# A hybrid decoder layer on one core: the up-projection by Strassen's seven products of quarters

## The chip, the core and the metric

The kernel runs on one core of a Trainium2 chip. A core has TensorE (PE: matmuls; PEld are its weight loads, which overlap them), VectorE (DVE), ScalarE (ACT), GpSimd (POOL) and SyncE (SP), which here issues nearly all DMAs. Each engine works through its own instructions in the order of the program and waits for others by semaphores. The metric is the device time of one execution in microseconds (us); lower is better.

## The reference, cut to what matters

One decoder layer is applied to a prompt of 2048 positions and a sample group of 8 x 4 positions, with shared weights. Everything is fp32. The change concerns the first matmul of the channel mixer:

```python
def conv_glu_ffn(x, conv_state, w_up, conv_w, conv_b, w_down):
    L = x.shape[1]
    a, g = jnp.split(x @ w_up, 2, axis=-1)        # w_up: 1024 x 5632
    ext = jnp.concatenate([conv_state.astype(a.dtype), a], axis=1)
    conv = conv_b
    for j in range(CONV_W):                        # CONV_W = 3
        conv = conv + ext[:, j:j + L] * conv_w[j]
    h = jax.nn.gelu(conv) * g
    return h @ w_down, ext[:, -(CONV_W - 1):]      # w_down: 2816 x 1024
```

Before it come a projection, a state-space scan, windowed attention, gates and a first layer norm; after it a second layer norm.

## The kernel before, in words

**Blocks.** The prompt is worked on in four blocks of 512 positions (`body`); block 1 also carries the 32 sample positions and has 544 columns. In each block the activations lie transposed (channels on partitions, positions along the row), so a weight tile of 128 x 128 is the stationary operand and 512 positions are the moving one.

**fp32 by three passes.** Every operand of a large matmul is split into a high part and the remainder, and a product is hi x hi + hi x lo + lo x hi. For weights, `Weights` does this: a *weight unit* is a tile of 128 x 1024 fp32 (512 KB); SP loads it into `wr` (3 buffers, line 192), ScalarE copies it to `wh`, and VectorE, or GpSimd for every third unit (line 202), subtracts to get `wl` (4 buffers each). `W.get` and `W.ahead` issue loads up to four units and splits up to three units ahead of the unit in use. `ws_unit` (line 226) issues a unit's matmuls (line 235).

**The channel mixer.** The 2816 channels are 22 *units* f of 128. Per f one weight unit makes the a half (`ua`) and one the g half (`ug`), 24 matmuls each (8 slices of the contraction x 3 passes). `ffn_tail` does the convolution (ScalarE's first tap and two VectorE operations) and gelu (square, a VectorE operation, tanh, a VectorE operation); between the two it calls `meanwhile`, which splits a weight unit. `ffn_gate` multiplies by g, splits a weight unit, and then splits the result into `hh` (ScalarE) and `hl` (VectorE). The f go in two groups, (0, 12) and (12, 22); after each the down-projection (`dn`, lines 239 to 241) takes the h of two f per weight unit and adds into z, once for each half of the 1024 output columns. `first_units` runs f = 0 and 1 in halves of 256 columns, because the positions of the second half are normalised later; `x1_evict` makes x1h and x1l, the parts of the normalised x1, by way of `x1f`.

**What sets the order.** The program's order is each engine's order. `Background` holds small steps with due times in *ticks*; `bg.tick()` is called after each weight unit or so and emits what is due: attention, the scan, tables, the rewriting of the residual rows by gain and bias (`x1_rows`, four GpSimd operations a row tile), the next block's input. In block 0 GpSimd also makes the scan's tables.

**Buffers.** All activations share one pool of 61 slots in SBUF; PSUM has 8 banks.

Of the kernel before, what the change touches and what calls it, by code (L numbers as in the profile page):

```python
# [8 lines left out]
F32 = mybir.dt.float32  # L9
# [15 lines left out]
SLOTS = 61  # L25
FU = 2
GROUPS = ((0, 12), (12, 22))
# [20 lines left out]
class Background:  # L48


    def __init__(self):
        self.now = 0
        self.todo = []
        self.n = 0
# [12 lines left out]
    def tick(self):  # L67
        due = sorted((x for x in self.todo if x[0] <= self.now), key=lambda x: (x[3], x[0], x[1], x[2]))
        self.todo = [x for x in self.todo if x[0] > self.now]
        self.now += 1  # L70
        for x in due:
            x[4]()

    def drain(self):
        while self.todo:
            self.tick()
# [3 lines left out]
def tile_hybrid_layer(ctx: ExitStack, tc: tile.TileContext,  # L80
# [4 lines left out]
    nc = tc.nc  # L85
# [47 lines left out]

    def unit_src(key):
# [27 lines left out]
        if k == "ug":  # L162
            return u_cols(w_up, 0, 8, DFF + key[1] * 128, 128)
        if k == "dn":
            return u_cols(w_down, (GROUPS[key[1]][0] + 2 * key[3]) * 128, 2, key[2] * 512, 512)
# [3 lines left out]
    for b in range(NBLK):  # L169
# [8 lines left out]
        for g, (f0, f1) in enumerate(GROUPS):  # L178
            for f in range(f0, f1):
                order += [("ua", f), ("ug", f)]  # L180
            order += [("dn", g, h, i) for h in range(2) for i in range((f1 - f0) // 2)]
# [1031 lines left out]
    def body(B, nxt):  # L1213
# [238 lines left out]
        x1l = {k: S("x1l", 544, F32R) for k in range(8)}  # L1452
        tps = {}
# [34 lines left out]
        def x1_evict(half):  # L1488
# [7 lines left out]
            f = [S("x1f") for _ in range(4)]  # L1496
            fk = lambda k: f[k // 2][:, (k % 2) * 256:(k % 2) * 256 + c]
# [40 lines left out]
        acc3 = wo_second(3)  # L1538
        upper, whole, lower = x1_evict(0)
# [22 lines left out]
        for i in range(B.nt):  # L1562
            bg.add(6 + 3 * i, lambda i=i: x1_rows(i))
        fst = Blk()

        def ffn_tail(f, pa, meanwhile):
# [3 lines left out]
            for i, c0, c in segs:  # L1570
                act(ae[:, 2 + c0:2 + c0 + c], pa[i][:, 0:c])
            G.tensor_copy(cc[:, :, f], ae[:, 512:514])  # L1572
# [5 lines left out]
            if B.sp:  # L1578
# [3 lines left out]
                act(ex[:, 16:48], pa[1][:, 256:288])  # L1582
# [5 lines left out]
            meanwhile()  # L1588
# [5 lines left out]
            fst.c = c_  # L1594
# [10 lines left out]
        def first_units():  # L1605
# [48 lines left out]
        for g, (f0, f1) in enumerate(GROUPS):  # L1654
# [8 lines left out]
            for f in range(f0 or 2, f1):  # L1663
                wa = [w.rearrange("p (k m) -> p k m", k=8) for w in W.get(("ua", f))]
                pa = ws_unit(*wa, 8, x1h, x1l, cols)
                ffn_tail(f, pa, W.ahead)
                bg.tick()
                wg = [w.rearrange("p (k m) -> p k m", k=8) for w in W.get(("ug", f))]
                pg = ws_unit(*wg, 8, x1h, x1l, cols)
                hh[f], hl[f] = ffn_gate(f, pg, W.ahead)  # L1670
                bg.tick()
            if g == 1:
                x1h.clear()
                x1l.clear()
                if nxt is not None:
# [9 lines left out]
                bg.add(3, lds)  # L1685
            for h in range(2):
# [14 lines left out]
                def dn_evict(t):  # L1701
# [7 lines left out]
                    if g == 1:  # L1709
# [4 lines left out]
                outer = 4 if B.last and g == 1 and h == 1 else 0  # L1714
                for i in range(nu - outer):
                    w = get(i)
                    for t in range(B.nt):
                        dn_mm(t, i, w)
                        if i == nu - 1:
                            dn_evict(t)  # L1720
                    bg.tick()
                if outer:
                    four = [get(nu - 4 + i, i) for i in range(4)]
                    for t in range(B.nt):
                        for i in range(4):
                            dn_mm(t, nu - 4 + i, four[i])
# [38 lines left out]

    B = new_block(0)
# [69 lines left out]
```

## Time and profile before

| | us |
|---|---|
| median of 3 runs | 2919.1 (2919.03 to 2923.91) |
| the profiled execution's own time | 2920.97 |
| its span, from the first to the last instruction | 2919.2 |

| engine | busy us | share |
|---|---|---|
| TensorE's weight loads | 2420.9 | 83% |
| VectorE | 1697.6 | 58% |
| ScalarE | 1142.5 | 39% |
| GpSimd | 1049.9 | 36% |

How to read it: busy time is the union of an engine's instructions over the span. Matmuls are pipelined, so the duration of one is longer than the distance to the next; the pace is read from starts or from counts in a stretch. PEclk is the granted share of TensorE's full clock. In a timeline, what stands in brackets behind a row is how long the engine was idle before it and what ended that.

### The profile page before, as it was taken

How to read it: one execution, taken by the hardware profiler on the slowest of the kernel's cores; microseconds unless marked ns; L12 is line 12 of the kernel's file. 1: busy time of each engine (PE TensorE's matmuls, PEld its weight loads, DVE VectorE, ACT ScalarE, POOL GpSimd, SP SyncE). 2: the span in 40 equal slices, each digit the busy share in tenths (PEclk: the TensorE clock that was granted, in tenths of full speed). 3: DMA queues.
4: the chain of work that ended last, by engine and by line, in shares of the span. 5: the costliest groups of instructions: out<-in, count | busy, mean ns of one | idle time of the engine just before them, and what ended most of it. 6: DMA issues, size and time to landing. Idle time of an engine off the chain costs nothing.

```text
span 2919.2 us, 39248 instructions
## 1 busy us (share of the span) xinstructions
PE 2843.7 (97%) x15168; PEld 2420.9 (83%) x15168; DVE 1697.6 (58%) x2678; ACT 1142.5 (39%) x1991; POOL 1049.9 (36%) x1098
## 2 busy tenths in 40 slices
PE   9899999999989999999999999999999999999998
PEld 8777888888888989989977778888888787888887
DVE  6975676254685447734646754673545853575365
ACT  3335344243326325423524442442433263344241
POOL 1955144111454313522217641351124651253122
PEclk9989999999999999999999999999999999999999
DMA  4422323234622242222325224233245423323232
GB/s 138 148 62 73 123 88 107 91 94 139 186 68 87 68 132 73 88 94 75 121 89 187 80 73 145 73 101 101 87 137 154 124 71 116 101 87 108 87 94 97
DMA packets 415118, 304.31 MB, mean 104 GB/s; under 512 B 52283, under 2 KB 351122, under 8 KB 414914
## 3 DMA queue, kind: packets, MB, share of 16 engines
q1 hardware_dynamic: 412114, 293.84, 33.0%
q0 software_dynamic: 2816, 7.96, 0.7%
q8 instruction: 119, 1.95, 0.3%
q14 instruction: 69, 0.57, 0.1%
HBM read 285.30 MB, written 17.39 MB: 104 GB/s over the span
## 4 chain that ended last, share of the span: by engine, by line
PE 82%; POOL 7%; DVE 6%; issue 2%; ACT 2%; DMA 0%; SPq 0%; POOLq 0%; DVEq 0%; ACTq 0%
PE ps L235 52%; PE ps L239 8%; PE ps L241 8%; PE ps L240 8%; PE ps L286 2%; POOL m L121 2%; POOL w L121 1%; PE ps L932 1%; POOL ht L121 1%; DVE m L121 1%; DVE m L776 1%; DVE wl L121 1%; POOL wl L121 1%; PE ps L247 1%; DVE x1l L121 0%
## 5 line engine op out<-in xcount | busy, mean ns | idle before, releaser
L121 POOL TENSOR_TENSOR wl<-wr,wh 128x1024 fp32r<-128x1024 f32 x144 | 358.5, 2490 | 991.1 <-ACT wh L113 957.9
L113 ACT ACTIVATE wh<-wr 128x1024 fp32r<-128x1024 f32 x448 | 470.4, 1052 | 292.3 <-PE ps L241 195.4
L235 PE MATMUL ps<-x1l,wh 128*128 128x512 f32 (+2 forms) x1856 | 569.4, 342 | 2.0 <-DVE x1l L121 2.0
L235 PE MATMUL ps<-x1h,wh 128*128 128x512 f32 (+2 forms) x1856 | 568.9, 342 | 0.0
L235 PE MATMUL ps<-x1h,wl 128*128 128x512 f32 (+2 forms) x1856 | 568.1, 341 | 0.0
L121 DVE TENSOR_TENSOR wl<-wr,wh 128x1024 fp32r<-128x1024 f32 x304 | 395.2, 1302 | 234.4 <-ACT wh L113 233.5
L235 PEld LDWEIGHTS ps<-x1l,wh 128*128 128x128 f32 x1856 | 326.4, 188 | 44.9 <-DVE x1l L121 3.0
L235 PEld LDWEIGHTS ps<-x1h,wl 128*128 128x128 f32 x1856 | 325.7, 188 | 41.8
L235 PEld LDWEIGHTS ps<-x1h,wh 128*128 128x128 f32 x1856 | 326.0, 188 | 41.3
L235 PE MATMUL ps<-xh,wh 128*128 128x512 f32 (+1 forms) x880 | 287.5, 358 | 11.7 <-DVE q L121 5.5
L235 PE MATMUL ps<-xh,wl 128*128 128x512 f32 (+1 forms) x880 | 281.6, 353 | 1.5 <-DVE wl L121 1.5
L235 PE MATMUL ps<-xl,wh 128*128 128x512 f32 (+1 forms) x880 | 281.8, 353 | 0.0
L239 PE MATMUL ps<-wh,hh 128*128 128x512 f32 x704 | 279.3, 397 | 0.0
L241 PE MATMUL ps<-wh,hl 128*128 128x512 f32 x704 | 277.9, 395 | 0.0
L240 PE MATMUL ps<-wl,hh 128*128 128x512 f32 x704 | 277.2, 394 | 0.0
L118 DVE SCALAR_TENSOR_TENSOR cv<-ae,pc,cv 128x512 f32<-128x512 f32 x176 | 145.7, 828 | 223.3 <-ACT cv L115 220.2
L235 PEld LDWEIGHTS ps<-xh,wh 128*128 128x128 f32 x880 | 157.7, 190 | 36.8 <-issue 5.9
L1572 POOL COPY cc<-ae 128x2 f32<-128x2 f32 x88 | 19.7, 224 | 468.1 <-ACT ae L113 467.3
L235 PEld LDWEIGHTS ps<-xh,wl 128*128 128x128 f32 x880 | 156.9, 190 | 25.4 <-DVE wl L121 2.5
L235 PEld LDWEIGHTS ps<-xl,wh 128*128 128x128 f32 x880 | 157.9, 190 | 20.9
L125 POOL TENSOR_SCALAR pp<-pp,su 128x256 f32<-128x256 f32 x128 | 143.6, 1139 | 84.0 <-DVE su L904 48.5
L239 PEld LDWEIGHTS ps<-wh,hh 128*128 128x128 f32 x704 | 132.7, 188 | 31.0
(363 smaller groups left out, 4966.4 us busy)
## 6 DMA issues: line engine op xcount, KB each, us to landing
wr<-in_w_up SPq DMA_DIRECT2D x176, 512.0 KB
wr<-in_w_in SPq DMA_DIRECT2D x88, 512.0 KB
wr<-in_w_down SPq DMA_DIRECT2D x88, 512.0 KB
wr<-in_w_glu SPq DMA_DIRECT2D x64, 256.0 KB
wr<-in_w_o SPq DMA_DIRECT2D x32, 512.0 KB
xin<-in_x_prompt SPq DMA_DIRECT2D x32, 256.0 KB
wr<-in_w_in SPq DMA_DIRECT2D x32, 256.0 KB
wr<-in_w_attn_br SPq DMA_DIRECT2D x32, 256.0 KB
```

The costliest lines, as they stand in the source:

```text
L113: A.activation(out, in_, AF.Copy, scale=scale, **kw)
L118: eng.scalar_tensor_tensor(out, a, s, b, op0=op0, op1=op1, **kw)
L121: eng.tensor_tensor(out, a, b, op=op)
L125: eng.tensor_scalar(out, a, s1, None, op0=op0)
L235: T.matmul(ps[:, :n], w[:, k, :], x[k][:, c0:c0 + n], start=(i == 0), stop=(i == len(ops) - 1))
L239: T.matmul(ps[:m], ah, wh, start=first, stop=False)
L240: T.matmul(ps[:m], ah, wl, start=False, stop=False)
L241: T.matmul(ps[:m], al, wh, start=False, stop=last)
L247: T.matmul(ps[:64], a, wh, start=first, stop=last)
L286: T.transpose(out, in_, ident[:k, :k])
L776: V.tensor_tensor_scan(v2[:, a, r, :], r4[:, gp:gp + 1].to_broadcast([128, 128]), v1[:, a, r, :], hc[:, r, gp:gp + 1], OP.mult, OP.add)
L932: T.matmul(B.ops[qb][r, :], vt[:, qb + kt, r], pt[kt], start=(kt == 0), stop=(kt == 1))
```

## The change

For 20 of the 22 units (f = 2 to 21) the up-projection of two neighbouring units becomes one *pair*. Its weights, 1024 x 256 for a and for g, are cut into quarters (halves of the contraction by the two units), the positions into two halves of 256 (272 in block 1); of the eight products of quarters Strassen's algorithm (the Winograd form) makes seven, three of plain quarters and four with sums of weights and of activations. A product takes one weight unit (its a and g parts, 4 slices each) and gives two PSUM banks of 256 columns; VectorE adds the products up. The sums of weights are made once, in the first ticks of the program, and kept in DRAM; the sums of x1 are made in each block by GpSimd and split like other operands. The activation tails of a pair are cut into six steps, which are emitted one per product of the next pair, or in the down-projection. There are four groups in place of two, and 65 slots.

```diff
-SLOTS = 61
+SLOTS = 65
-GROUPS = ((0, 12), (12, 22))
+GROUPS = ((0, 6), (6, 12), (12, 16), (16, 22))
+LG = len(GROUPS) - 1
+PRODUCTS = ("11", "21", "t4", "t1", "t2", "t3", "22")
...
+    def tick(self, draining=False):
...
+        if not draining:
+            next(self.steps, None)
...
+    def up_part(f, what, h):
+        r0, c0 = 512 * (what[0] == "2"), h * DFF + (f + (what[1] == "2")) * 128
+        return w_up[r0:r0 + 512, c0:c0 + 128].rearrange("(k p) m -> p k m", p=128)
+
+    def weight_sums():
+        for f in range(2, NF, 2):
+            for h in range(2):
+                v = {}
+                for what in ("11", "12", "21", "22"):
+                    v[what] = S("ws")
+                    SP.dma_start(v[what].rearrange("p (k m) -> p k m", k=4), up_part(f, what, h))
+                yield
+                tt(v["11"], v["12"], v["11"], OP.subtract, G)
+                tt(v["12"], v["22"], v["12"], OP.subtract, G)
+                tt(v["22"], v["22"], v["11"], OP.subtract, G)
+                tt(v["21"], v["21"], v["22"], OP.subtract, G)
+                yield
+                yield
+                for what, src in (("t1", "11"), ("t3", "12"), ("t2", "22"), ("t4", "21")):
+                    SP.dma_start(sums[f, what][:, h * 512:(h + 1) * 512], v[src])
+                del v
+                yield
...
-            bg.add(6 + 3 * i, lambda i=i: x1_rows(i))
+            bg.add(3 + 3 * i, lambda i=i: x1_rows(i))
...
+        def x1_sums():
+            for k in range(4):
+                s12, s34 = S("s12", 544), S("s34", 544)
+                lo_, hi_ = slice(0, hn), slice(hn, n)
+                tt(s12[:, lo_], x1f[k][:, hi_], x1f[k + 4][:, hi_], OP.add, G)
+                tt(s12[:, hi_], s12[:, lo_], x1f[k][:, lo_], OP.subtract, G)
+                tt(s34[:, lo_], x1f[k][:, lo_], x1f[k][:, hi_], OP.subtract, G)
+                tt(s34[:, hi_], x1f[k + 4][:, lo_], s12[:, hi_], OP.subtract, G)
+                for j, t in enumerate((s12, s34)):
+                    sh[j, k], sl_[j, k] = split(B, t, None, "s")
...
+        def tail():
+            if tails:
+                tails.pop(0)()
+
+        def pair(f):
...
+            for i in range(7):
+                hi, lo = (w.rearrange("p (h k m) -> p h k m", h=2, k=4) for w in W.get(("up", f, i)))
+                xh_, xl_ = operand(i)
+                ps[i] = [P()[:, 0:hn] for _ in range(2)]
+                for h in range(2):
+                    ws_unit(hi[:, h], lo[:, h], 4, xh_, xl_, [(0, hn)], ps[i][h:h + 1])
+                for h in range(2):
+                    c11, c12, c21, c22 = out(h, 0, 0), out(h, 1, 0), out(h, 0, hn), out(h, 1, hn)
+                    u = u2[:, h * hn:(h + 1) * hn]
+                    p_ = ps[i][h]
+                    if i == 0:
+                        act(u, p_)
+                    elif i == 1:
+                        tt(c11, u, p_, OP.add)
+                    elif i == 4:
+                        tt(u, u, p_, OP.add)
+                        tt(c12, u, ps[3][h], OP.add)
+                        tt(c21, u, ps[2][h], OP.add)
+                    elif i == 5:
+                        tt(c22, c12, p_, OP.add)
+                        tt(c21, c21, p_, OP.add)
+                    elif i == 6:
+                        tt(c12, c12, p_, OP.add)
...
+                W.ahead()
+                tail()
+                bg.tick()
...
+            for i in range(2):
+                tails.extend((lambda i=i: convolved(i), activated, lambda i=i: gated(i)))
...
                     for fn in x1_evict(1):
                         fn()
+                    x1_sums()
                 half0(i)
...
-            for f in range(f0 or 2, f1):
...
+            for f in range(f0 or 2, f1, 2):
+                pair(f)
...
-                        bg.add(2 + k, lambda k=k: x_split(nxt, k))
+                        bg.add(2 + k // 2, lambda k=k: x_split(nxt, k))
-                bg.add(3, lds)
+                bg.add(1, lds)
...
                         if i == nu - 1:
                             dn_evict(t)
+                    for _ in range(-(-6 // (nu - 1))):
+                        tail()
                     bg.tick()
...
+    bg.steps = weight_sums()
```

`convolved` is the convolution of `ffn_tail`, `activated` its gelu, and `gated` the multiplication by g and the split of `ffn_gate`; the weight splits that lay inside these functions are now in `W.ahead`, once per product. `x1f` is kept for whole rows until the sums are made. In the last block all steps of the last half down-projection, not four of five, are held and run position tile by position tile. The scratch space for DMA descriptors is set to 4096, which makes room for the slots.

## Rows read from the trace of the kernel before

**Rows 1.** The page's first part: busy us (share of the span) xinstructions, by engine.

```profile
PE 2843.7 (97%) x15168; PEld 2420.9 (83%) x15168; DVE 1697.6 (58%) x2678; ACT 1142.5 (39%) x1991; POOL 1049.9 (36%) x1098
```

**Rows 2.** Table of stretches: us, busy us and instructions by engine, PEclk, DMA share, GB/s.

```profile
2060.00:2160.00 100.00, 100.00 (x436) 81.35 (x435) 59.13 (x67) 47.39 (x64) 21.15 (x23) 1.00 0.34 105
2590.00:2670.00 80.00, 80.00 (x349) 65.03 (x348) 59.19 (x56) 38.26 (x52) 39.28 (x32) 1.00 0.34 104
2690.00:2742.00 52.00, 52.00 (x225) 42.06 (x224) 10.52 (x12) 9.54 (x9) 7.34 (x4) 1.00 0.29 91
...
1370.00:1450.00 80.00, 80.00 (x643) 80.00 (x642) 49.94 (x79) 39.00 (x72) 17.57 (x28) 1.00 0.29 89
```

**Rows 3.** Timeline of PE in the first units: start us, us, instruction.

```profile
2548.51 0.28 PE L235 MATMUL ps<-x1h,wh 128*128 128x256 f32 x1
...
2549.22 0.28 PE L235 MATMUL ps<-x1h,wh 128*128 128x256 f32 x1
```

**Rows 4.** The page's groups, weight loads: xcount, busy us, mean ns, idle before.

```profile
L235 PEld LDWEIGHTS ps<-x1l,wh 128*128 128x128 f32 x1856 | 326.4, 188 | 44.9 <-DVE x1l L121 3.0
```

**Rows 5.** Timeline of VectorE, additions of 256 columns from PSUM.

```profile
810.54 0.42 DVE L121 TENSOR_TENSOR m<-ps,tber 128x256 f32<-128x256 f32 x1
810.88 0.41 DVE L121 TENSOR_TENSOR m<-ps,tbei 128x256 f32<-128x256 f32 x1
```

**Rows 6.** Timelines of ScalarE and VectorE over one unit's tail, block 3.

```profile
2574.71 0.82 ACT L115 ACTIVATE cv<-ae,pc 128x512 f32<-128x512 f32 x1 [1.40 <-POOL ae L1569]
2577.13 0.63 ACT L115 ACTIVATE cq<-cv 128x512 f32<-128x512 f32 x1 [1.61 <-DVE cv L118]
2578.52 0.63 ACT L115 ACTIVATE cq<-cq 128x512 f32<-128x512 f32 x1 [0.76 <-DVE cq L118]
2579.06 1.04 ACT L113 ACTIVATE wh<-wr 128x1024 fp32r<-128x1024 f32 x1
2580.71 0.63 ACT L113 ACTIVATE hh<-cv 128x512 fp32r<-128x512 f32 x1 [0.60 <-DVE cv L118]
...
2575.56 1.54 DVE L118 SCALAR_TENSOR_TENSOR cv<-ae,pc,cv 128x512 f32<-128x512 f32 x2 [0.93 <-ACT cv L115]
2577.80 0.69 DVE L118 SCALAR_TENSOR_TENSOR cq<-cq,cv 128x512 f32<-128x512 f32 x1 [0.70 <-ACT cq L115]
2579.19 0.69 DVE L118 SCALAR_TENSOR_TENSOR cv<-cq,cv 128x512 f32<-128x512 f32 x1 [0.70 <-ACT cq L115]
2579.99 0.69 DVE L118 SCALAR_TENSOR_TENSOR cv<-cv,ps 128x512 f32<-128x512 f32 x1
2580.59 1.22 DVE L121 TENSOR_TENSOR wl<-wr,wh 128x1024 fp32r<-128x1024 f32 x1
2581.73 0.69 DVE L121 TENSOR_TENSOR hl<-cv,hh 128x512 fp32r<-128x512 f32 x1
```

**Rows 7.** Timelines of GpSimd and VectorE, block 2.

```profile
2085.08 2.40 POOL L121 TENSOR_TENSOR wl<-wr,wh 128x1024 fp32r<-128x1024 f32 x1 [5.60 <-ACT wh L113]
...
2086.26 1.76 DVE L121 TENSOR_TENSOR hl<-cv,hh 128x512 fp32r<-128x512 f32 x1 [0.70 <-ACT hh L113]
```

**Rows 8.** Groups by form, GpSimd, whole span.

```profile
L121 POOL TENSOR_TENSOR x1l<-x1f,x1h 128x256 fp32r<-128x256 f32 x16 | 14.2, 919 | 0.0
```

**Rows 9.** Table of stretches, mixer of block 0.

```profile
66.00:141.00 75.00, 71.02 (x423) 61.58 (x422) 69.68 (x104) 25.07 (x45) 70.24 (x110) 1.00 0.48 144
141.00:200.00 59.00, 48.18 (x236) 41.86 (x235) 53.39 (x78) 14.79 (x21) 39.23 (x49) 0.83 0.27 86
```

**Rows 10.** The page's third part: DMA queue, kind: packets, MB, share of 16 engines.

```profile
q1 hardware_dynamic: 412114, 293.84, 33.0%
```

**Rows 11.** Timeline of PE around a wait in block 2, and the table of stretches there.

```profile
1542.71 0.40 PE L239 MATMUL ps<-wh,xh 128*128 128x512 f32 x1
1548.50 0.81 PE L240 MATMUL ps<-wl,xh 128*128 128x512 f32 x1 [5.39 <-POOL wl L121]
...
1545.00:1552.00 7.00, 3.50 (x9) 2.88 (x10) 0.16 (x1) 0.00 (x0) 6.74 (x8) 0.51 0.33 92
```

More of the change, by code (lines that the diff above doesn't have):

```diff
@@ L51, in __init__ @@
     def __init__(self):
+        self.steps = iter(())
         self.now = 0
@@ L132, in u_cols @@
                            w[r0:r0 + 128 * kk, c0:c0 + m].rearrange("(k p) m -> p k m", p=128))]
+    sums = {}
+    for f in range(2, NF, 2):
+        for what in ("t1", "t2", "t3", "t4"):
+            sums[f, what] = dram.tile([128, 1024], F32, name=f"sum_{f}_{what}")
+    def up_part(f, what, h):
+        r0, c0 = 512 * (what[0] == "2"), h * DFF + (f + (what[1] == "2")) * 128
+        return w_up[r0:r0 + 512, c0:c0 + 128].rearrange("(k p) m -> p k m", p=128)
+    def weight_sums():
+        for f in range(2, NF, 2):
+            for h in range(2):
[14 more added lines that the diff above has]
+                yield
     def unit_src(key):
@@ L163, in unit_src @@
             return u_cols(w_up, 0, 8, DFF + key[1] * 128, 128)
+        if k == "up":
+            f, what = key[1], PRODUCTS[key[2]]
+            if what[0] == "t":
+                return lambda t: [(t, sums[f, what])]
+            return lambda t: [(t.rearrange("p (h k m) -> p h k m", h=2, k=4)[:, h], up_part(f, what, h))
+                              for h in range(2)]
         if k == "dn":
@@ L178, in tile_hybrid_layer @@
         for g, (f0, f1) in enumerate(GROUPS):
-            for f in range(f0, f1):
-                order += [("ua", f), ("ug", f)]
+            if g == 0:
+                order += [(n_, f) for f in range(2) for n_ in ("ua", "ug")]
+            for f in range(f0 or 2, f1, 2):
+                order += [("up", f, i) for i in range(7)]
             order += [("dn", g, h, i) for h in range(2) for i in range((f1 - f0) // 2)]
@@ L1495, in x1_evict @@
             sl = slice(c0, c0 + c)
-            f = [S("x1f") for _ in range(4)]
-            fk = lambda k: f[k // 2][:, (k % 2) * 256:(k % 2) * 256 + c]
+            fk = lambda k: x1f[k][:, sl]
             def affine(out, k):
@@ L1538, in body @@
         acc3 = wo_second(3)
+        x1f.update({k: S("x1f", 544) for k in range(8)})
         upper, whole, lower = x1_evict(0)
@@ L1571, in ffn_tail, with conv @@
                 act(ae[:, 2 + c0:2 + c0 + c], pa[i][:, 0:c])
+            conv(f, ae, pa[1][:, 256:288] if B.sp else None)
+            meanwhile()
+            fst.c = gelu(fst.c)
+        def conv(f, ae, own):
             G.tensor_copy(cc[:, :, f], ae[:, 512:514])
@@ L1662, in body @@
                 first_units()
-            for f in range(f0 or 2, f1):
[L1664 to L1672, printed above, removed]
+            for f in range(f0 or 2, f1, 2):
+                pair(f)
+            if g == LG:
                 x1h.clear()
                 x1l.clear()
+                sh.clear()
+                sl_.clear()
                 if nxt is not None:
@@ L1713, in body @@
                 get = lambda i, held=0: [w.rearrange("p (k m) -> p k m", k=2) for w in W.get(("dn", g, h, i), held)]
-                outer = 4 if B.last and g == 1 and h == 1 else 0
+                outer = nu if B.last and g == LG and h == 1 else 0
                 for i in range(nu - outer):
```

52 lines of the change are left out of this document (42 added, 10 removed).

## The prediction, made before the changed kernel ran

> **What bounds the kernel now.** I read the page's first part before anything else: TensorE is busy for 2843.7 of 2919.2 us, and no other engine passes 58% [rows 1]. Then I took the table of stretches over the up-projection: in the late stretch of block 2 TensorE is full, VectorE works 59 us of 100; in the early one of block 3, where GpSimd rewrites the residual rows, VectorE works 59.2 of 80 [rows 2]. So TensorE sets the pace here, and a change that takes matmul columns away pays only until VectorE's queue becomes the slower one. That queue has to be read next, in order of time, since each engine works strictly in the order of the program.
>
> **TensorE's part.** A pair of units costs 4 x 24 = 96 matmuls of 512 columns now; the late stretch and the down-projection stretch give 0.229 and 0.231 us from one to the next [rows 2], so 96 x 0.230 = 22.1 us. After it costs 7 x 2 x 12 = 168 matmuls of 256 columns. The first two units already run such matmuls, each with weights of its own: 0.71 us for six, 0.118 us each [rows 3]. 168 x 0.118 = 19.8 us, 2.26 less. Ten pairs in three blocks: 67.8 us. In block 1 the same 544 columns run as 256 + 288: 80 us for 643 matmuls [rows 2], 0.1244 at a mean of 272 columns, which is just the new width: 192 x 0.1244 = 23.9 before, 168 x 0.1244 = 20.9 after, ten times 2.99 = 29.9. Together **-97.7 us**, and nothing else in the change gives time back.
>
> A rule of the Trainium skill speaks against this step: TensorE: Matmul & The Clock Gate, Part 3 (What overlaps and what doesn't), has a weight load overlap a running matmul only when it goes to another row group, and its section on LDWEIGHTS gives the columns over 1.2, about 107 ns for 128. By it each of the 72 more loads of a pair would cost 107 ns, an estimate of 7.7 us a pair, more than the columns save. The rows say otherwise: 0.118 us at 256 columns is only 3 ns above half of 0.230, though each load there lasts 0.188 [rows 4], so the loads are hidden. The measurement decides.
>
> **VectorE in the pairs.** All starts below are spaced some 0.08 us closer than the durations, as queued neighbours show (0.42 long, 0.34 apart [rows 5]).
> - Splitting weights: seven units instead of four a pair, two thirds on VectorE; 1.22 long, 1.14 to the next [rows 6]: 4.67 x 1.14 = 5.3 us.
> - Combining products: 14 additions of 256 columns from PSUM, nearest row 0.34 apart [rows 5]: 4.7 us.
> - The two activation tails: each 1.54 for two taps and four operations of 0.69 [rows 6]: 8.6 us.
> That is 18.6 us, beside 19.8 of TensorE. But a tail step is now emitted without anything between its halves: VectorE waits 0.70 for ScalarE's tanh and again 0.70 for its hh [rows 6], 2.8 us a pair, which in the kernel before cost nothing. And GpSimd's third of the splits is not free: while it makes one (2.40), VectorE's hl with both inputs in SBUF takes 1.76 and not 0.69 [rows 7]; 2.33 such splits a pair cost up to 2.5 us. A pair that carries the tails of the pair before needs 21.4 to 23.9 us of VectorE, 1.6 to 4.1 over TensorE. Weights are split two to three units ahead, so the first such pair of a group loses little, the second all. Six of ten pairs carry tails (the first of each group doesn't): four lose 1, two lose 4: **+12 us a block** (0 if waits and lengthening vanish, 6 x 4.1 = 25 if nothing is buffered). ScalarE needs 7 splits of 1.04 [rows 6] and some 5 us of tails: 12 of 19.8, no bound. The ae and cc copies keep their count. Weights on SP need 7 x 1.7 = 12 us of the queue a pair (the 1.7 below), hidden under the products; the loads of g2 and b2 and the next block's splits, moved a few ticks, stay under the last group's down-projection, where every engine but TensorE is mostly idle [rows 2].
>
> **The ends of the groups.** This is the largest term. The last pair's six tail steps begin only when its last product is evicted, and run beside the down-projection, whose last unit needs both results. One unit's chain is in the trace link by link: ScalarE's first tap starts at 2574.71, the gate product ends at 2580.68, hh at 2581.34, and hl would take 0.69 more but for the split queued ahead of it [rows 6]: 7.4 us; the second unit follows in the same queues, its first tap (0.85) done in advance: 6.5. With the eviction (0.8) and one weight split (1.14): 15.8 us. Cover: a down unit is 24 x 0.231 = 5.55 us [rows 2]. Groups of three steps hide 11.1 + 0.7 us, a wait of 4.0; the group (12, 16) has two, hides 6.2, a wait of 9.6. That is 21.6 us a block even if VectorE arrives on time. It arrives late by what its pairs lag, up to some 6 us where splits and evictions are still queued; I take 14 over the four ends: **+36 a block** (ends 21 and 43). The kernel before has none of this: its gate came one unit later and the results five steps before their use. The 16 more evictions into z a block are hidden: VectorE works 10.5 of 52 us there [rows 2].
>
> **The head of the block.** x1_sums puts 16 GpSimd additions of 256 columns (nearest row 0.92 [rows 8], 14.7 us) and 8 splits ahead of the first units' tails; ScalarE and VectorE stand behind GpSimd in them. TensorE has six half units, 6 x 24 x 0.118 = 17 us, until the first pair wants weights that are split after that. The row rewriting, three ticks earlier, follows on GpSimd. The bounds are 0 (all covered) and 15 (none); nearest is the early stretch, where such work lengthens VectorE most [rows 2]: **+9 a block**.
>
> **The weight sums, in block 0 alone.** Twenty rounds of four ticks: 2 MB of loads and stores on SP, four GpSimd additions. 11 rounds lie before the up-projection, where GpSimd is busy 70 of 75 us and, just after, TensorE waits for it (PE 48 of 59 us, clock 0.83) [rows 9]; a round's 5 us land there twice: 0 to 12 us. Nine rounds fall into the up-projection. Queue q1 moved 293.84 MB in 33.0% [rows 10], so 1.7 us for 512 KB: four ticks need 4 x 1.7 for weights and 6.9 for the sums, 13.8 us, against four products of 11.3. Stores wait for GpSimd in SP's queue, the weight loads behind them, and the pair's splits behind those: with 2.5 us short in every four ticks, and up to 1.7 more each time that SP stands, 0 to 38 us over nine rounds. I take **+35** in all.
>
> **The clock.** After a wait of 5.4 us the next matmul took 0.81, and the clock stood at 0.51, the lower of its two levels (1.2 GHz, not 2.4), for that stretch of 7 us [rows 11]; 3.5 us of work at half speed is 1.75 lost. Sixteen group ends could cost 28 us (0 if the waits come in pieces, 40 with the heads); **+20**.
>
> **The sum**, against the profiled execution's own 2920.97 us (span 2919.2; 1.9 over the median 2919.1, no difference, since 0.2%, 6 us, is about what can be told from no change): -97.7 + 4 x (12 + 36 + 9) + 35 + 20 = +185: **3106 us**. Its own range, with half the way to either bound in each term, is 3020 to 3170.
>
> **Rivals.**
> - *Light:* little lengthening by GpSimd, small lags. Group ends 26, pairs 4, head 3 a block, sums 20, clock 10: -97.7 + 132 + 30 = +64: 2985. For it: the 36 us are built on lags that no row shows.
> - *Heavy:* 43, 18 and 14 a block, sums 50, clock 30: -97.7 + 300 + 80 = +282: 3203. For it: GpSimd is shared by sums, rows, splits at the head, and the lags add up.
> - *VectorE keeps pace (not slower):* the place is the first down matmul on a last pair's h. If tailed pairs need under 19.8 us of VectorE, nothing lags, only the 21.6 us a block of the bare chain stay: -97.7 + 86 = -12: 2909. It decides at 19.8; the 2.8 us of waits and the 1.76 speak against it, TensorE's full stretches for it.
> - *Weight loads show:* 72 more loads a pair at 0.188 [rows 4], 13.5 us, 40 pairs, +541; VectorE then keeps up, and 2909 becomes 3450. The 0.118 is against it. This is the case that the Trainium skill's rule above (TensorE: Matmul & The Clock Gate, Part 3) describes.
>
> **Numbers.** 3106: 0.45; light 0.22; heavy 0.21; pace 0.10; loads 0.02. The range 2950 to 3215 leaves out pace, loads and heavy's upper part. Faster: 0.08, same 0.03 (both of pace), slower 0.89.
>
> **What would show it.** Matmuls of 256 columns 0.118 apart in the pairs' products. TensorE waiting for hl and hh of the last pair at every group's end, longest at (12, 16). VectorE over 90% in second and third pairs, and waits for wl there. Block 0's up-projection longer than block 2's, with SP waiting for GpSimd. If VectorE's share stays below 85% in tailed pairs and the waits at group ends are under 4 us, the forecast is wrong, and the time is near or below 2920.

## The result, and the profile after

The changed kernel takes 3268.1 us (median; 3264.3 to 3270.7) against 2919.1: a ratio of 1.119 [1.117, 1.121]. The direction was right, but the time lies 53 us above the upper end of the range, 162 above the forecast, and above the rival *heavy* (3203). Differences between kernels below are differences of such ratios, times 2919 us. The profiled execution has a span of 3262.5 us.

The page's first part of the changed kernel, which answers [rows 1]:

```profile
PE 2871.5 (88%) x17088; PEld 2523.1 (77%) x17088; DVE 2142.5 (66%) x3402; ACT 1254.1 (38%) x2123; POOL 1340.4 (41%) x1282
```

TensorE has fallen from 97% to 88% and no other engine is near full: the time is waiting. Whom TensorE waited for (us in total, times, longest), cut after six lines but for the last states' (L279 is the matmul line of the up-projection and the mixer, L283 the first one of the down-projection, L330 the transposes):

```profile
PE ps L283 <- ACT hh L119: 137.8, 30, 7.2
PE ps L279 <- DVE u L127: 65.2, 24, 7.1
PE ps L279 <- POOL wl L127: 50.2, 25, 11.7
PE ps L847 <- POOL ht L127: 21.0, 9, 4.2
PE ps L279 <- DVE wl L127: 18.6, 18, 3.4
PE ps L279 <- ACT wh L119: 15.2, 5, 5.3
PE ps L330 <- ACT hco L119: 10.3, 1, 10.3
```

The first is the group ends, the second the pairs, the third mostly the head of a block, the fourth the mixer of block 0, where the kernel before waits 16.4 us in the same place. The table of stretches shows where they lie in block 3 (us, busy us and instructions of PE, PEld, DVE, ACT, POOL, then PEclk, DMA share, GB/s): the first group's up-projection, then the second group's first pair, its two pairs with tails, and its down-projection:

```profile
2804.30:2896.50 92.20, 70.89 (x546) 69.12 (x545) 66.21 (x88) 38.77 (x56) 66.76 (x57) 0.91 0.32 103
2942.50:2962.30 19.80, 19.80 (x169) 19.80 (x168) 12.24 (x19) 7.97 (x9) 5.15 (x4) 1.00 0.52 160
2962.30:2986.60 24.30, 21.46 (x170) 21.28 (x169) 17.25 (x23) 10.19 (x15) 5.97 (x4) 0.93 0.44 135
2986.60:3010.40 23.80, 20.94 (x171) 20.31 (x170) 20.45 (x31) 11.65 (x16) 7.55 (x6) 1.00 0.47 151
3010.40:3056.00 45.60, 36.27 (x145) 28.21 (x145) 23.56 (x33) 14.38 (x18) 8.14 (x7) 0.89 0.29 93
```

The pair without tails is the 19.8 us of the forecast to the tenth; a pair with tails costs 24; the down-projection stands 9 us and runs partly at half clock.

### The profile page after: what moved, and what is told of

It reads as the page before. It is cut to its first block, busy times and chain, and to the rows that moved or that the text cites. A ratio compares the mean times of both kernels' runs of the same rounds, so it can differ in the third digit from the quotient of the medians.

```text
span 3262.5 us, 45363 instructions
## 1 busy us (share of the span) xinstructions
PE 2871.5 (88%) x17088; PEld 2523.1 (77%) x17088; DVE 2142.5 (66%) x3402; ACT 1254.1 (38%) x2123; POOL 1340.4 (41%) x1282
## 4 chain that ended last, share of the span: by engine, by line
PE 53%; DVE 21%; POOL 11%; ACT 7%; issue 6%; DMA 2%; SPq 0%; POOLq 0%; DVEq 0%; ACTq 0%
PE ps L279 30%; DVE cv L124 8%; PE ps L283 6%; PE ps L284 6%; PE ps L285 6%; DVE wl L127 4%; ACT wh L119 2%; ACT cq L121 2%; PE ps L330 2%; POOL s L127 2%; POOL wl L127 2%; POOL m L127 2%; DVE cq L124 2%; POOL xr L127 1%; DVE ae L127 1%
## 5 line engine op out<-in xcount | busy, mean ns | idle before, releaser
L127 DVE TENSOR_TENSOR wl<-wr,wh 128x1024 fp32r<-128x1024 f32 x384 | 526.9, 1376 | 212.8 <-ACT wh L119 204.7
L279 PE MATMUL ps<-sh,wh 128*128 128x256 f32 (+1 forms) x1280 | 378.1, 295 | 69.2 <-DVE u L127 65.2
L283 PE MATMUL ps<-wh,hh 128*128 128x512 f32 x704 | 299.7, 426 | 137.8 <-ACT hh L119 137.8
L279 PE MATMUL ps<-sh,wl 128*128 128x256 f32 (+1 forms) x1280 | 377.3, 295 | 34.9 <-POOL wl L127 30.7
L279 PE MATMUL ps<-sl,wh 128*128 128x256 f32 (+1 forms) x1280 | 374.4, 292 | 0.0
L279 PE MATMUL ps<-x1h,wl 128*128 128x256 f32 (+2 forms) x1216 | 338.1, 289 | 31.9 <-POOL wl L127 19.5
L279 PE MATMUL ps<-x1h,wh 128*128 128x256 f32 (+2 forms) x1216 | 336.9, 288 | 14.1 <-ACT wh L119 14.0
L279 PE MATMUL ps<-x1l,wh 128*128 128x256 f32 (+2 forms) x1216 | 338.8, 289 | 6.4 <-DVE x1l L127 6.4
L279 PEld LDWEIGHTS ps<-sh,wh 128*128 128x128 f32 x1280 | 254.9, 199 | 74.2 <-issue 69.7
L279 PE MATMUL ps<-xh,wh 128*128 128x512 f32 (+1 forms) x880 | 288.8, 360 | 10.0 <-DVE q L127 3.8
L279 PE MATMUL ps<-xh,wl 128*128 128x512 f32 (+1 forms) x880 | 284.2, 356 | 2.2 <-DVE wl L127 2.2
L279 PEld LDWEIGHTS ps<-sh,wl 128*128 128x128 f32 x1280 | 255.0, 199 | 39.0 <-POOL wl L127 33.4
L279 PE MATMUL ps<-xl,wh 128*128 128x512 f32 (+1 forms) x880 | 284.2, 356 | 0.0
L283 PEld LDWEIGHTS ps<-wh,hh 128*128 128x128 f32 x704 | 142.9, 203 | 182.1 <-ACT hh L119 151.1
L279 PEld LDWEIGHTS ps<-x1h,wl 128*128 128x128 f32 x1216 | 228.7, 193 | 36.9 <-POOL wl L127 22.1
L279 PEld LDWEIGHTS ps<-sl,wh 128*128 128x128 f32 x1280 | 255.2, 199 | 0.0
L279 PEld LDWEIGHTS ps<-x1h,wh 128*128 128x128 f32 x1216 | 229.7, 193 | 16.4 <-ACT wh L119 15.0
L279 PEld LDWEIGHTS ps<-x1l,wh 128*128 128x128 f32 x1216 | 230.2, 193 | 10.1 <-DVE x1l L127 9.4
```

The source lines that it names most:

```text
L127: eng.tensor_tensor(out, a, b, op=op)
L279: T.matmul(ps[:, :n], w[:, k, :], x[k][:, c0:c0 + n], start=(i == 0), stop=(i == len(ops) - 1))
L283: T.matmul(ps[:m], ah, wh, start=first, stop=False)
```

## The experiments

**What the stages cost against their own grouping.** `e1_groups` gives the kernel before the four groups and nothing else; its row rewriting keeps its old ticks and so comes behind the first evictions into z of the last rows (its output is not the reference's).

```diff
-GROUPS = ((0, 12), (12, 22))
+GROUPS = ((0, 6), (6, 12), (12, 16), (16, 22))
...
-                        bg.add(2 + k, lambda k=k: x_split(nxt, k))
+                        bg.add(2 + k // 2, lambda k=k: x_split(nxt, k))
...
```

> The kernel before, with nothing of the seven products: only its units are done in the four groups (0,6), (6,12), (12,16), (16,22), the next block's splits and the loads of g2 and b2 a few ticks earlier as in the change. Theory (the time is TensorE's short waits, made by the tails that lie behind the last product): the gate comes one unit later here as before, so a group's end waits little: 0 to +10 us on 2919. Rival 'grouping' (sixteen more evictions into z and shorter down-projections cost the time by themselves): +40 a block, some 3080.

Ratio 1.0027 [1.0016, 1.0039], +8 us: the rival falls. Its stages are now the measure for the changed kernel's, since they have the same borders. Block 3's first group, second group's up- and down-projection:

```profile
2546.00:2617.60 71.60, 69.23 (x402) 60.43 (x401) 54.38 (x66) 35.17 (x51) 36.00 (x34) 1.00 0.32 96
2650.80:2717.20 66.40, 66.40 (x289) 54.01 (x288) 37.10 (x42) 29.11 (x39) 13.56 (x15) 1.00 0.29 88
2717.20:2750.70 33.50, 33.50 (x146) 27.16 (x145) 11.90 (x15) 8.48 (x9) 4.93 (x4) 1.00 0.36 111
```

Added up from the first matmul of each stage to the first of the next, over the four blocks (us):

| stage | e1 | changed | difference |
|---|---|---|---|
| first group's up-projection | 297.5 | 393.1 | +95.6 |
| later groups' up-projections | 725.4 | 743.7 | +18.3 |
| down-projections | 520.8 | 720.2 | +199.4 |
| mixer of block 0 | 363.2 | 386.9 | +23.7 |

By its columns alone TensorE would save 19.5 us in the first groups and 78.2 in the later up-projections. Against that, these stages and the down-projections are 115, 96 and 199 us too long. Of this TensorE's waits, less those of e1, are 86, 69 and 148 us, and the loss of its matmuls at half clock is some 19, 20 and 41; the remaining 10 or so in each are not accounted for.

**Cutting the suspected costs, one at a time.** `e2_nosums`: the sums are not made, t1 to t4 load plain quarters.

```diff
-    bg.steps = weight_sums()
-                return lambda t: [(t, sums[f, what])]
+                what = ('11', '12', '21', '22')[int(what[1]) - 1]
```

> The changed kernel without the weight sums: products t1 to t4 load plain quarters of w_up in place of the sums, so the same bytes and matmuls run and the output of the up-projection is not the reference's. Theory: block 0's mixer loses 23.6 us of waits and its FFN the 23 that it is longer than blocks 2 and 3: 3268 - 47 = 3221 (3205 to 3235), nothing in blocks 1 to 3. Rival 'SP holds the loads back in all blocks' (a sum's load is one transfer of 512 KB, a plain one two): 3268 within 10, or other blocks change too.

1.1022 [1.1005, 1.1038], -49: 24.6 us of it in block 0's mixer, 25 in its channel mixer (451.5 for 476.5), blocks 1 to 3 as they were. Theory held.

`e3_ends`: the last down unit takes earlier hh and hl.

```diff
+                        r = f - 2 if i == nu - 1 else f
...
-                            tok_mm(acc[t], hh[f][:, t * 128:t * 128 + m], hl[f][:, t * 128:t * 128 + m],
+                            tok_mm(acc[t], hh[r][:, t * 128:t * 128 + m], hl[r][:, t * 128:t * 128 + m],
```

> The changed kernel in which the last down unit of every group multiplies with hh and hl of the two units before, not with those of the group's last pair; the tails of the last pair are still computed, their results not used, so the output is not the reference's. Theory: waits of 156 us at the sixteen group ends go, with the half clock behind them (some 40 of the 82 us): 3268 - 196 = 3070 (3050 to 3110). Rival 'VectorE is the bound' (the work that TensorE waited for is only shifted: the next pair waits instead): under 60 us less, above 3200.

1.077 [1.0754, 1.0786], -123. The hh waits fell from 137.8 us to 13.1:

```profile
PE ps L279 <- DVE u L127: 62.0, 24, 7.0
...
PE ps L283 <- ACT hh L119: 13.1, 4, 5.0
```

The other stages kept their time (ups 744.6, first groups 395.4), so the rival falls as well. The theory's 196 us are not reached either. All waits in the down-projections fell from 148 us to 50, since 26 us of others took the place of hh's, and of the half clock there some 25 of 41 us came back. The last group's ends stay 5 to 12 us longer than e1's: the next block's input and the last states are transposed there, their copies out of PSUM stand on ScalarE and VectorE behind the tails, and TensorE waits for them (in block 3 10.3 us in one piece, as in the changed kernel).

`e4_nox1sums` and `e17_nohead`, the head of the block:

```diff
-                    x1_sums()
+                    x1f.clear()
...  e17 besides:
-        for i in range(B.nt):
-            bg.add(3 + 3 * i, lambda i=i: x1_rows(i))
```

> The changed kernel without x1_sums: products t1 to t4 take plain quarters of x1h and x1l, so 16 GpSimd additions, 8 splits a block are left out and the output is not the reference's; the rewriting of the rows stays. Theory: the waits at the head (35, 27, 21, 23 us in blocks 0 to 3, of which 2.9 each were there before) come mostly from this work: -15 to -20 a block with their clock, 3268 - 70 = 3200 (3180 to 3225). Rival 'the rows and the splits of weights on GpSimd make the head's waits': under 20 us less, about 3250.

1.1053 [1.1036, 1.1069], -40, between theory and rival; block 3's longest wait (8.2 us) stayed, so the additions are not the whole head.

> The kernel without x1_sums (3227.8), less the rewriting of the rows as well (the residual rows stay as normalised; the output is not the reference's). Theory 'GpSimd's queue at the head': the wait of 8.4 us for a wl on GpSimd and its neighbours go, -8 to -12 a block with their clock: 3180 to 3196. Rival 'loads or ScalarE hold these splits': within 12 us of 3228.

1.0909 [1.089, 1.0927], another -42; the first groups are down to 311.3 us from 393.1. GpSimd's timeline in the changed kernel, block 3, shows what TensorE waited for until 2869: a split of weights (`wl`) behind eight operations on the rows.

```profile
2849.65 2.38 POOL L127 TENSOR_TENSOR wl<-wr,wh 128x1024 fp32r<-128x1024 f32 x1 [5.28 <-ACT wh L119]
2851.99 1.75 POOL L127 TENSOR_TENSOR xr<-xr,g1t 128x512 f32<-128x512 f32 x1
2853.82 2.16 POOL L127 TENSOR_TENSOR xr<-xr,b1t 128x512 f32<-128x512 f32 x1
...
2864.58 2.12 POOL L127 TENSOR_TENSOR xr<-xr,b1t 128x512 f32<-128x512 f32 x1
2866.66 2.33 POOL L127 TENSOR_TENSOR wl<-wr,wh 128x1024 fp32r<-128x1024 f32 x1
```

And TensorE's, in the same place:

```profile
2869.05 0.58 PE L279 MATMUL ps<-sh,wl 128*128 128x256 f32 x1 [8.18 <-POOL wl L127]
```

`e7_rows` only moves the rows back by four ticks (`7 + 3 * i`).

```diff
-            bg.add(3 + 3 * i, lambda i=i: x1_rows(i))
+            bg.add(7 + 3 * i, lambda i=i: x1_rows(i))
```

> The changed kernel with the rewriting of the rows four ticks later (7, 10, 13, 16 in place of 3, 6, 9, 12), still before the first eviction into z. Theory: of the head's waits the longest (8.3 us in block 3, TensorE waiting for a wl that is queued on GpSimd behind the rows) goes, since the rows no longer follow straight on the 16 additions: -6 to -10 a block, 3232 to 3245. Rival: the rows only move the same wait to a later pair: within 10 us of 3268.

1.1177 [1.1161, 1.1194], -4, not told apart from none: the rival. The first groups are 13 us shorter and the down-projections 15 longer, so the cost moved.

`e8_out`: the cuts of e2, e3 and e4 at once.

```diff
...  the edits of e2_nosums, e3_ends and e4_nox1sums
```

> The changed kernel without the weight sums, without x1_sums (t1 to t4 take plain quarters on both sides) and with the last down unit of each group multiplying with the hh and hl of the two units before, all three at once; the output is not the reference's. If the three costs are separate (49.4, 40.3 and 122.6 us as single cuts gave): 3268 - 212 = 3056, and 137 over the kernel before remain for the pairs, the rows and the clock. Rival 'one queue behind all of them' (VectorE's or GpSimd's, so that one cut already gave part of another): 3080 or more. Rival 'they hid each other': under 3030.

1.0454 [1.0438, 1.0469], -215 where the single cuts give 212: three separate costs. It also shows that without these three costs the change is still 133 us slower than before.

**The pairs.** `e5_banks`: both halves of a product in one PSUM bank.

```diff
-                ps[i] = [P()[:, 0:hn] for _ in range(2)]
+                bank = P() if not B.sp else None
+                ps[i] = [P()[:, 0:hn] if B.sp else bank[:, h * hn:(h + 1) * hn] for h in range(2)]
```

> The changed kernel in which the two halves of a product (activation and gate) share one PSUM bank in blocks 0, 2 and 3 (in block 1 they don't fit), so a pair holds half as many banks and product 5 needs none that product 4 holds. The same work. Theory 'banks': TensorE's waits for VectorE's u (14.3, 23.4 and 11.6 us in these blocks) are waits for a bank; they go, with their half clock: -49 to -70, 3200 to 3220. Rival 'VectorE is the bound of a tailed pair': the wait moves to the next weights (wl) or the next evictions and the time stays within 15 us of 3268.

1.1224 [1.1207, 1.1241], +10: no gain; the waits for u went in blocks 0, 2 and 3, and those for wl and hh grew. The bank only sets where VectorE's lateness is felt.

`e6_wlv`: no weight split of a pair on GpSimd.

```diff
-                e = eng or (G if self.splits % 3 == 2 and self.splits > 24 else V)
+                e = eng or (G if self.splits % 3 == 2 and self.splits > 24 and order[self.splits][0] != "up" else V)
```

> The changed kernel with all weight splits of the pairs on VectorE, none on GpSimd (2.33 a pair more on VectorE at 1.14, 2.7 us). Theory 'GpSimd's queue and its slowing of VectorE' (hl 1.76 in place of 0.69 beside a GpSimd split): the POOL wl waits (24, 6, 5 and 19 us) go, the pairs stay as they are since what VectorE gets more it also loses in lengthening: -50 to -80, about 3205. Rival 'VectorE's load': tailed pairs get 2.7 us longer, six a block, +65, less the head's 55: about 3275.

1.108 [1.1062, 1.1099], -32, between the two: the later up-projections fall by 28 us, the first groups by 9. With 2.33 more splits a pair VectorE is busy for 17.26 and 20.45 us in the second group's tailed pairs of block 3, as it was in the changed kernel (17.25 and 20.45): it had lost as much beside GpSimd's splits.

```profile
2940.00:2963.00 23.00, 22.45 (x190) 22.28 (x190) 17.26 (x26) 11.04 (x15) 0.00 (x0) 1.00 0.49 153
2963.00:2986.90 23.90, 20.11 (x152) 19.53 (x151) 20.45 (x33) 11.85 (x18) 0.31 (x2) 0.93 0.47 143
```

The head gains little, though no split of a pair stands behind the rows any more. TensorE now waits 32 us in the four first groups for splits on VectorE (11 before, and 39 for GpSimd's), which take up to 2.28 us for 1.22 beside GpSimd's operations on the rows:

```profile
2830.09 2.28 DVE L127 TENSOR_TENSOR wl<-wr,wh 128x1024 fp32r<-128x1024 f32 x1
```

So the rows cost by GpSimd's queue and by slowing VectorE, and e17 doesn't tell the two apart. In the changed kernel's VectorE timeline, in a pair, the two taps (`cv`, x2) take 3.14 us, 1.54 in [rows 6].

```profile
2962.85 1.22 DVE L127 TENSOR_TENSOR wl<-wr,wh 128x1024 fp32r<-128x1024 f32 x1
2967.44 3.14 DVE L124 SCALAR_TENSOR_TENSOR cv<-ae,pc,cv 128x512 f32<-128x512 f32 x2 [3.37 <-ACT cv L121]
2970.50 0.42 DVE L127 TENSOR_TENSOR ae<-u,ps 128x256 f32<-128x256 f32 x1
...
2973.68 0.69 DVE L124 SCALAR_TENSOR_TENSOR cv<-cq,cv 128x512 f32<-128x512 f32 x1 [0.70 <-ACT cq L121]
...
2977.16 0.69 DVE L127 TENSOR_TENSOR hl<-cv,hh 128x512 fp32r<-128x512 f32 x1 [0.70 <-ACT hh L119]
...
2981.78 0.41 DVE L127 TENSOR_TENSOR u<-u,ps 128x256 f32<-128x256 f32 x1
```

The same rows show VectorE standing: 3.37 us, because ScalarE's first tap is emitted behind its copies of the pair's first product (and one of a weight), and 0.70 for tanh and for hh. TensorE waits 2.8 us for the u at 2981.78. Two kernels each take a part of these waits away by order alone. `e9_weave` (five steps, the two units interleaved) does it for tanh and hh (62 and 58 us in the whole kernel become 34 and 2, while those before the taps rise from 42 to 60):

```diff
-                tails.extend((lambda i=i: convolved(i), activated, lambda i=i: gated(i)))
+            tails.extend((steps((convolved, 0)), steps((squared, 0), (convolved, 1), (cubed, 0)),
+                          steps((squared, 1), (gated, 0), (cubed, 1)), steps((gated, 1), (hsplit, 0)),
+                          steps((hsplit, 1))))
```

> The changed kernel with the tails of a pair's two units woven together: five steps in place of six, each emitted one product later than the ScalarE result that it needs, so that VectorE no longer stands for tanh and hh; the same instructions. Theory 'VectorE is the bound in a tailed pair, and part of its time is waiting' (four waits of 0.70, 2.8 us a pair): six tailed pairs a block get up to 2.8 us shorter (-67 in four blocks), and the chain at a group's end, where the two units now overlap, 3 to 5 us (-48 to -80): 3130 to 3180. Rival 'its work alone fills it' (the waits are covered by lateness): under 30 us less, above 3240.

`e13_early` (a product's tail step ahead of its evictions) does it before the taps (42 us become 26):

```diff
+                tail()
                 for h in range(2):
...
                 W.ahead()
-                tail()
                 bg.tick()
```

> The changed kernel with each tail step emitted ahead of the evictions of its product in place of behind them; the same instructions. Theory 'order' (VectorE idles 3.4 us at the start of a tailed pair, since ScalarE's first tap stands in its queue behind the eviction of the pair's first product): conv runs while TensorE computes that product, six tailed pairs a block get 2 to 4 us shorter, with half clock behind the 3 us waits: -48 to -110, 3160 to 3220. Rival 'VectorE's work' (17 to 20 us busy, and 1.1 to 2 longer for each operation beside a GpSimd split): within 25 us of 3268.

1.1126 [1.111, 1.1143] and 1.1113 [1.1095, 1.1132], -19 and -23: the rival in both, and the stages say why. Weaving shortens the down-projections by 83 us and lengthens the up-projections by 53 (later) and 17 (first groups); early tails give -38, +12 and +7. VectorE does the tails sooner and is then late for the additions of the products: TensorE's waits for u in the later up-projections grow from 50 us to 83 (e9) and 57 (e13).

**The ends and the sum of the remedies.** `e10_both` puts both column halves' first units ahead of the two last ones, in the first three groups of blocks 0, 2 and 3.

```diff
+        return [(h, i) for h in range(2) for i in range(nu - 1)] + [(h, nu - 1) for h in range(2)]
...
-                for i in range(nu - outer):
+            for h, i in dn_seq(B.b, g):
```

> The changed kernel with another order of the down units: at the end of the first three groups of blocks 0, 2 and 3 both column halves' units but the last two run first, then the two last (8 PSUM banks), so 22 us of other products (11 at (12,16)) stand before the first use of the last pair's hh; everywhere the last unit takes all rows of its first h before the second. The same instructions. Theory (the ends are a chain of 20 us behind a cover of 11): of the waits of 9, 9 and 9.6 us at these nine ends all but some 5 at (12,16) go, with 1 us of half clock each, -75; the other seven ends lose 2 us each, -14: 3268 - 89 = 3180 (3160 to 3200). Rival 'VectorE's lag is carried over': what the end no longer waits, the next group's first pair waits: above 3230.

1.0892 [1.0874, 1.091], -87, as expected: the down-projections fall by 94 us, the other stages keep their time (+4).

`e12_all` is e6, e9 and e10 together; `e14_early_all` e6, e10 and e13; `e15_early_weave` all four.

```diff
...  the edits of e6_wlv and e10_both, with e9_weave (e12), e13_early (e14) or both (e15)
```

> The woven tails, the new order of the down units and all weight splits of the pairs on VectorE together, on the changed kernel; all of it computes what the change computes. If the three are separate: 3268 - 34 (as measured for the splits) - 100 - 89 = 3045; the two that shorten the ends overlap, so 3060 to 3110 is expected. What is left over the kernel before is then the weight sums (49), x1_sums (40) and VectorE's tailed pairs: it does not get under 2919 in either theory.

1.081 [1.0792, 1.0827], -111, 50 to 100 us short of what was expected, since weaving gave so little.

> Tail steps ahead of the evictions, the new order of the down units and all pair splits on VectorE together. If early gives what 'order' expects (say 80) and adds: 3268 - 80 - 84 - 34 = 3070; with splits and early sharing a part 3070 to 3110. If 'VectorE's work' holds: 3150.

1.0646 [1.063, 1.0662], -159 where the three give 142 singly: the best version that computes the reference, still 189 us above the kernel before. No experiment points to one that beats it; the seven products with fewer groups, and so fewer ends, were not run.

> The same with the woven tails besides. If weaving lengthened the pairs only because its heavier steps stood before product 4's evictions, this does it again: e14's time + 0 to 20. If the waits for tanh and hh are what is left: 15 to 40 us under e14.

1.0682 [1.0666, 1.0698], +11 over e14, inside the 0 to 20 of the first case, but not in its place: in the later up-projections TensorE's waits for u stay (28 us for 30), those for weight splits grow (27 for 12). VectorE's waits for ScalarE in the tails are 52 us here and 148 in e14: they are not what sets the pair.

`e16_taps` takes work off VectorE in e14:

```diff
-            stt(c_[:, 0:512], ae[:, 1:513], w(1), c_[:, 0:512], OP.mult, OP.add)
-            stt(c_[:, 0:512], ae[:, 2:514], w(2), c_[:, 0:512], OP.mult, OP.add)
+            if f < 2:
+                stt(c_[:, 0:512], ae[:, 1:513], w(1), c_[:, 0:512], OP.mult, OP.add)
+                stt(c_[:, 0:512], ae[:, 2:514], w(2), c_[:, 0:512], OP.mult, OP.add)
```

> The version with tail steps first, the new order of the down units and all pair splits on VectorE (3110.5), less the two convolution taps on VectorE of each unit from the third on: 3.1 us of VectorE a pair; the output is not the reference's. Theory 'VectorE's work sets a tailed pair': its 23.3 us (three pairs with two tailed in 66.4) fall by about 3, to TensorE's own 20 to 20.5, six a block, with some of the half clock: -60 to -90, 3020 to 3050. Rival 'waits and order set it': the three-pair stages keep 65 us and more, under 25 us less in all.

1.0349 [1.0332, 1.0366], -87 from e14: what no reordering did in the pairs, less work does. But only 35 us of it are in the later up-projections and 12 in the first groups. The other 36 are in the down-projections, where the chain to hh is shorter without the taps, which the theory hadn't counted; that the time fell into its range is partly luck. In the pairs it is the work: in e14 VectorE stood only 10.5 us before all taps of the kernel together, so their wait was gone already. The second group's three pairs in block 3, in e14 and in e16:

```profile
2815.50:2881.80 66.30, 62.07 (x506) 61.31 (x505) 52.13 (x82) 31.39 (x42) 0.86 (x6) 0.97 0.49 153
```

```profile
2754.20:2815.90 61.70, 60.37 (x506) 60.00 (x505) 46.17 (x73) 30.00 (x40) 0.86 (x6) 1.00 0.53 163
```

61.7 us is 2.3 above three pairs of TensorE at 19.8.

**The clock.** `e11_fill` puts matmuls that nobody reads into the waits at the ends.

```diff
+                        if i == nu - 1 and h == 0 and t == 0 and kk == 1:
+                            for _ in range(22):
+                                T.matmul(fill, hh[f0][:, 0:128], hh[f0][:, 0:512], start=True, stop=True)
```

> The changed kernel with 22 matmuls of 512 columns (5.1 us at full clock), whose results nobody reads, in front of the last unit's second h at each of the sixteen ends, where TensorE waits 5.2 to 6.9 us: they fill the wait and nothing else changes. Theory 'the clock falls because TensorE stands, and costs some 1 us an end': the half clock behind the ends goes, -10 to -25: 3243 to 3258. Rival 'the clock's loss lies elsewhere (head, pairs)': within 8 us of 3268. If the filled wait was no wait: up to +60.

1.1143 [1.1126, 1.116], -14 by the ratios (-8 by the medians, -2 by the profiled spans): inside what the theory gave for the ends, and small. Cores view, the changed kernel and e11:

```profile
core 0: 3262.5 us, clock 0.943
```

```profile
core 0: 3260.7 us, clock 0.955
```

Clock 0.943 means 372 us at half clock (2 x 0.057 x 3262.5), in 52 stretches by the trace's clock records, 40 of them in the channel mixers (300 us); the kernel before had 11 (59 us in all), one of them there. In the four channel mixers the matmuls that start at clock 0.50, waits left out, follow each other 84 us later, in sum, than at full clock (0.230 for 512 columns, 0.118 for 256). In e11 that is 67 us for the matmuls whose results are used, and 13 for the idle ones. So filling the waits took some 80 us of half clock off and about 17 of lost time, which fits the 14 of the ratios: most of those stretches were ones in which TensorE stood. At most ends a wait of some 2.7 us was left, and half clock follows most of these too.

## Why the prediction was wrong, step by step

The mechanism was right: VectorE and GpSimd make TensorE wait in the pairs, at the ends and at the head. What failed are the sizes of three terms: the clock (79 us for 20), the tailed pairs (96 for 40 in the later groups) and the head (82 for 36), the last two with the clock in them.

- **TensorE, -97.7: right.** 168 matmuls of 256 columns in 19.80 us, at 0.118, with 168 weight loads hidden. The rival *weight loads show* fell. The rule of the Trainium skill that stood for it (TensorE: Matmul & The Clock Gate, Part 3) does not hold here: the untailed pair's row has a load for each matmul and no time for it.
- **VectorE in the pairs, +12 a block: mis-sized, and with it the statement on buffering.** The price of a tailed pair, 1.6 to 4.1 us, was right at its upper end (24.3 and 23.8 for 19.8). The step that failed is "four lose 1, two lose 4": a group's first tailed pair loses as much as its second (4.5 and 4.0 here). Its reason was that weights are split ahead, but TensorE waits there mostly for the additions of the products (u, 50 of 69 us), which nothing splits ahead. The later groups' up-projections are 18 us longer than e1's where TensorE alone would make them 78 shorter (32 pairs), so they lose 96 us, some 20 of it the clock, for 40 (five of the six tailed pairs of a block are there). That VectorE would show over 90% was wrong (71 and 86%): it is late and idle in turn, since it works in order. Yet e16 shows that its work sets most of a tailed pair's excess in e14 (4.6 of 6.9 us in three pairs), and e5 and e15 that the bank and its waits for ScalarE don't.
- **Lengthening beside GpSimd, part of the same term: right in kind.** The Trainium skill (GPSIMD Engine Reference, 8. Key points) has GpSimd contend with VectorE's instructions with two SBUF inputs; the rows agree (taps 3.14 for 1.54, while the 84 additions from PSUM that ran beside a GpSimd split took 0.42 as ever). By e6 it costs some 2.7 us a pair, for the up to 2.5 of the forecast: 2.33 splits of 1.14 more left VectorE's busy time as it was.
- **The ends of the groups, +36 a block: right, 37 in waits.** TensorE waits 148 us in the sixteen down-projections, longest in (12, 16), for 144; since 14 of the 36 were a guess about lags, that nearness is partly luck. The down-projections are 199 us longer than e1's because 51 more come from matmuls at a slower pace, 41 of them lost at half clock: that is the clock's term. e3 ties 123 us to the last pair's hh; e10, which lengthens the cover, takes 87 off. One step was put at nothing and was not: the next block's input and the last states under the last group's down-projection, which was read off a down-projection without tails [rows 2], are queued behind tails. It is 30 us in e3, where hh is out of the way; in the changed kernel TensorE's waits show 10.3 of it.
- **The head, +9 a block: mis-sized, a step that failed.** x1_sums alone costs 40 us (e4), the rows 42 more (e17), 82 with the clock for 36. In e1, with the rows, TensorE waits only 9.5 us in all first groups. The upper bound of 15 was the 14.7 us of additions (16.8 in block 3's trace). That the rows follow on GpSimd was named and not priced: they hold back GpSimd's weight splits, up to eight operations ahead of one, and slow VectorE's (e6). That they came three ticks earlier matters little (e7).
- **The weight sums, +35: 49**, at the upper bound of 50, half in the mixer and half in the channel mixer of block 0, as described; SP stood 98.5 us for the sums on GpSimd.
- **The clock, +20: the most mis-sized term.** It is some 79 us (84, less 5 that e1 has too), over the bound of 40. The 1.75 us per wait was near (84 us over 40 stretches is 2.1); the count was not: only the sixteen ends were counted, and 20 us taken, but waits of some 3 us in the pairs and of up to 8 and more at the head bring half clock too, and an end often has two.

With the clock inside its stages: -98 + 96 + 199 + 98 (head: the first groups' 95.6 and the 19.5 us that TensorE saves there, less the 17 of the sums; one tailed pair a block is in it) + 49 + 8 (grouping) = +352, for 343 between the spans. 8 of the sums' 49 lie in block 0's later stages and are counted twice.

The rivals *light* and *VectorE keeps pace* fell with the pairs; *heavy* had the mechanism and stopped 65 us short, mostly at the clock (30 for 79) and the head.

## What to carry over

Work taken off the full engine is worth only what the next queue in order leaves of it: here VectorE went from 13 us in the time of two units (59.13 of 100 [rows 2], over 22.1) to 17 to 20 in a pair, and of the stages with tails only the two-pair ones of (12, 16) gained anything on e1 (1.5 to 5 us, in three of the four blocks). Before spreading a tail over the next stage, add up per stage what the second engine must do, at its contended durations, and count every place where the full engine will stand 3 us, since each also cost some 2 us of half clock here. Where a result is due at the end of a stage, other work of the full engine put in between (e10, -87) was worth more than getting the chain done sooner (e9 and e13, -19 and -23), which lengthened the up-projections by 70 and 19 us for the 83 and 38 that it saved in the down-projections.

## What the runs showed of the hardware

- Beside one GpSimd split a VectorE operation of 512 columns with two SBUF inputs took 2.71 us for 0.69 (an hl in e9, beside a split of 2.63): it can be held up for most of the GpSimd instruction.
- Behind waits of some 3 us TensorE's clock already stood at 0.50 (the pair at 2962, whose only long wait is one of 2.8 us, has 0.93 in its row). In the changed kernel's channel mixers half clock followed each of the 35 waits of 3 us or more and 12 of the 18 between 2 and 3 us. Keeping TensorE busy with idle matmuls in the longer waits at the ends brought back at most 14 us.
